# A large and a small expert by turns: eight MoE experts computed as four pairs, on one Trainium2 core

## The chip, the cores and the metric

One core of a Trainium2 chip runs the whole program, one launch. The metric is the device time of a run in microseconds (us). Engines are named as the profile names them: PE is TensorE (PEld its weight loads), DVE is VectorE, ACT is ScalarE, POOL is GpSimd, SP is SyncE, which issues the weight transfers.

## What is computed

A two-layer diffusion backbone on 256 context and 256 latent tokens of width 1024. The change lies in the last part of layer 1, a mixture of eight experts of which every latent token takes the best two. Each expert has three weight matrices in float32, 1024 x 2816 for gate and up, 2816 x 1024 for down:

```python
def swiglu(h, w_gate, w_up, w_down):
    return (jax.nn.silu(h @ w_gate) * (h @ w_up)) @ w_down

def moe_swiglu(h, router_w, w_gate, w_up, w_down):
    logits = (h @ router_w).astype(F32)
    top_v, top_i = lax.top_k(logits, TOP_K)
    top_w = jax.nn.softmax(top_v, axis=-1)
    combine = jnp.sum(jax.nn.one_hot(top_i, N_EXPERTS, dtype=F32) * top_w[..., None], axis=-2)
    out = jnp.zeros(h.shape[:-1] + (w_down.shape[-1],), h.dtype)
    for e in range(N_EXPERTS):
        out = out + combine[..., e:e + 1].astype(h.dtype) * swiglu(h, w_gate[e], w_up[e], w_down[e])
    return out
```

## The kernel before

Expert 0 and the three fullest of the others get 128 token slots, the other four get 64; a ranking on the chip decides which of experts 1 to 7 is computed in which place. Places 0, 2, 4, 6 are the large ones (`expert`), places 1, 3, 5, 7 the small ones (`expert64`). Place 2p and place 2p+1 are pair p. What the program calls expert `e` is a place; `home_of(e)` reads the number of the real expert into a register of SP, whose DMAs use it as address.

**Weights.** Each place takes 33 loads of 128 x 2048 float32 (1 MB): 22 for gate and up, 11 for down. `load` issues them from SP into ten buffers in rotation: seven called `raw`, two `own`, one `whole`. The tile `whole` also holds the small expert's tokens (`xs`) and its activations (`a64`), so a row `whole<-pm` on ACT writes those.

**Large expert.** Six groups, five of four loads and one of two, each 512 (256) columns of gate and up. A load is split for precision in two halves, each into `whi` (ACT, L352) and the rest `wlo` (DVE, L353), three buffers of each, and a k-tile takes three matmuls: high x high, low tokens x high, high x low (L1196 to L1198). A group is 48 matmuls. Its result goes through Silu (ACT, L1201) and the product with up (DVE, L1202) into `a`; later `turned` transposes `a` (PE, L1207) and stores it as `ahi` (ACT, L1209) and `alo` (DVE, L1210). The down loads use the same split and three matmuls (L1232 to L1234) into two PSUM tiles `pd`, one for each half of the output columns.

**Small expert.** The same groups, but its matmuls (L1253) take the weights unsplit in float32, eight to a gate or up load and four to a down load (L1289), two of them beside each other in the array. Silu is L1259, the product L1260, the transposes L1265, their evacuation L1267.

**Around them.** `pick` makes the one-hot matrices of a pair, `gather` (L1147, four matmuls for each of eight k-tiles) collects the tokens of the next pair during the small expert's down loads, `scatter_rows` transposes the one-hots, `scatter` writes a half of an expert's output back: `y` (ACT, L1299, one buffer) and its rest (DVE, L1300), eight matmuls (L1305), four additions (L1308).

**Order.** The places are computed one after the other, all of place 0, then all of place 1, and so on. Which instruction stands where in an engine's list is decided when the program is built, by a scheduler that goes by priorities (the splits are marked high) and by its own estimate of when operands are there. Each engine then works through its list. SP issues the loads in the order of the program, each when its buffer is free.

Of the kernel before, what the change touches and what calls it, by code (L numbers as in the profile page):

```python
# [20 lines left out]
KD = 8  # L21
# [62 lines left out]
def host_layout(x, c, ctx, c_ctx, ada_w, ada_b, mix_norm_w, ffn_norm_w, w_in, hg_lb_logits, hg_norm_w,  # L84
# [95 lines left out]
    "pre": 4,  # L180
    "hold": 5,
    "ff": (1, 1),
    "sg": 1,
    "tt": 2,
    "td": 2,
    "slots": (3, 5, 8),
    "pk": 3,
    "gd": 1,
    "sd": 8,
    "dv": ([], [4, 5, 6, 7, 8, 9, 10, 11, 12, 13, 14, 15, 16, 17, 18]),  # L190
    "al": 2,
    "pc": ((), ()),
# [6 lines left out]
def tile_kernel(ctx: ExitStack, tc: tile.TileContext, xT, cT, cR, ada_w, w_in, w_br, w_out, ffn_gu, ffn_d, router,  # L199
# [29 lines left out]
    def pm(shape=(P, 512)):  # L229
        return pt("pm", n_pm, shape)  # L230
# [928 lines left out]
    def scatter_rows(pr, oh):  # L1159
        ohf = oh.bitcast(F32)  # L1160
        pw = pm((P, 2))
        ws = mt((2,), "ws", 2)
        pt_ = pm((P, 2, 2, P))
        oT = mt((2, 2, P), "oT", 1, F32R)
        for ee in range(2):
            for t in range(2):
                T.matmul(pw[:, ee:ee + 1], ohf[:, t, ee], wgt_s[:, t, 2 * pr + ee:2 * pr + ee + 1],
                         start=t == 0, stop=t == 1)
                T.transpose(pt_[:, ee, t], ohf[:, t, ee], ident)
        V.tensor_copy(ws, pw)  # L1170
        S.activation(oT, pt_, AF.Copy)
        return ws, oT

    def expert(e, oh, st, choose, early):
        pr, ee = divmod(e, 2)
        at_ = home_of(e)
        if ee:
            return expert64(e, at_, oh, st, choose, early)
        xv = [xg[:, s_] for s_ in range(2)]
        aT, turn_ = [], []  # L1180
        for g in range(6):
            w = 512 if g < 5 else 256
            kc = 4 if g < 5 else 8
            pss = []
            for u in range(2):
                ps = pj() if g % 2 else pt(("po", "pa")[u], 1)
                for c in range(8 // kc):
                    n = 4 * g + 2 * u + c if g < 5 else 20 + u
                    raw = load(moe[at_, n]).rearrange("p (k c) -> p k c", k=kc)
                    for k0 in range(0, kc, kc // 2):  # L1190
                        if turn_ and 4 * (kc * c + k0) >= kc * PLAN["tt"]:
                            turn_.pop()()
                        hi, lo = split(raw[:, k0:k0 + kc // 2], (kc // 2, w))
                        for k in range(kc // 2):
                            kk = kc * c + k0 + k
                            T.matmul(ps[:, :w], xv[0][:, kk], hi[:, k], start=kk == 0, stop=False)  # L1196
                            T.matmul(ps[:, :w], xv[1][:, kk], hi[:, k], start=False, stop=False)  # L1197
                            T.matmul(ps[:, :w], xv[0][:, kk], lo[:, k], start=False, stop=kk == 7)  # L1198
                pss.append(ps)
            a = tpool.tile([P, 512], F32, tag="rstd", name=nm("act"))  # L1200
            S.activation(a[:, :w], pss[0][:, :w], AF.Silu)  # L1201
            V.tensor_tensor(a[:, :w], a[:, :w], pss[1][:, :w], ALU.mult)  # L1202

            def turned(a=a, nt=w // P):
                pq = pm((P, 4, P))
                for q in range(nt):
                    T.transpose(pq[:, q], a[:, q * P:(q + 1) * P], ident)  # L1207
                hi, lo = mt((4, P), "ahi", 6, F32R), mt((4, P), "alo", 6, F32R)
                S.activation(hi[:, :nt], pq[:, :nt], AF.Copy)  # L1209
                V.tensor_tensor(lo[:, :nt], pq[:, :nt], hi[:, :nt].bitcast(F32), ALU.subtract)  # L1210
                aT.append((hi, lo))

            turn_.append(turned)
            if g == PLAN["pk"]:
                choose()
            if g == PLAN["sg"]:
                if late:
                    late.pop()()
                st.update(zip(("ws", "oT"), scatter_rows(pr, oh)))
        pd = [pm(), pm()]  # L1220
        for c in range(11):
            raw = load(moe[at_, 22 + c]).rearrange("p (k c) -> p k c", k=4)
            early(c - PLAN["gd"])
            for k in range(4):
                h_, kk = DOWN[4 * c + k]
                if turn_ and 4 * c + k == 2 * PLAN["td"]:
                    turn_.pop()()
                if k % 2 == 0:
                    hi, lo = split(raw[:, k:k + 2], (2, 512))
                ahi, alo = (x[:, kk % 4] for x in aT[kk // 4])  # L1230
                first, last = (kk == 0, kk == 21) if h_ == 0 else (kk == 20, kk == 19)
                T.matmul(pd[h_], ahi, hi[:, k % 2], start=first, stop=False)  # L1232
                T.matmul(pd[h_], alo, hi[:, k % 2], start=False, stop=False)  # L1233
                T.matmul(pd[h_], ahi, lo[:, k % 2], start=False, stop=last)  # L1234
            if c == PLAN["sd"]:
                scatter(e, 0, pd[0], st["ws"], st["oT"])
        late.append(lambda: scatter(e, 1, pd[1], st["ws"], st["oT"]))

    def expert64(e, at_, oh, st, choose, early):


        aT, turn_ = {}, []
        for g in range(6):
            w = 512 if g < 5 else 256
            kc, hw = (4 if g < 5 else 8), w // 2
            ps = pj((P, 2, 256))
            for u in range(2):
                for c in range(8 // kc):
                    raw = load(moe[at_, 4 * g + 2 * u + c if g < 5 else 20 + u]).rearrange("p (k c) -> p k c", k=kc)
                    for k in range(kc):  # L1250
                        kk = kc * c + k
                        for h_ in range(2):
                            T.matmul(ps[64 * h_:64 * h_ + 64, u, :hw], xs[:, kk], raw[:, k, h_ * hw:(h_ + 1) * hw],  # L1253
                                     start=u + kk == 0, stop=u == 1 and kk == 7, tile_position=(0, 64 * h_),
                                     skip_group_check=True)
                    if turn_:
                        turn_.pop()()
            a = tpool.tile([P, 512], F32, tag="rstd", name=nm("act"))[:, :hw]
            S.activation(a, ps[:, 0, :hw], AF.Silu)  # L1259
            V.tensor_tensor(a, a, ps[:, 1, :hw], ALU.mult)  # L1260

            def turned(a=a, g=g, nt=hw // P):
                pq = pm((P, 4, P))
                for q in range(nt):
                    T.transpose(pq[:, q], a[:, q * P:(q + 1) * P], ident)  # L1265
                o = a64[:, g]
                S.activation(o[:, :nt], pq[:, :nt], AF.Copy)  # L1267
                for h_ in range(2):
                    for q in range(nt):
                        aT[4 * g + nt * h_ + q] = o[:, q, 64 * h_:64 * h_ + 64]  # L1270

            turn_.append(turned)
            if g == PLAN["pk"]:
                choose()
            if g == PLAN["sg"] and late:
                late.pop()()
        if e == NE - 1:
            S.activation(mt((1,), "most"), a[:, 0:1], AF.Exp, scale=0.0)
        pd = [pm(), pm()]
        for c in range(11):  # L1280
            raw = load(moe[at_, 22 + c]).rearrange("p (k c) -> p k c", k=4)
            early(c - PLAN["gd"])
            for k in range(4):
                h_, kk = DOWN[4 * c + k]
                if turn_ and c == 1:
                    turn_.pop()()
                r = kk % 2
                first, last = (kk < 2, kk >= 20) if h_ == 0 else (kk >= 20, 18 <= kk < 20)
                T.matmul(pd[h_][64 * r:64 * r + 64], aT[kk], raw[:, k], start=first, stop=last,  # L1289
                         tile_position=(0, 64 * r), skip_group_check=True)  # L1290
            if c == PLAN["sd"]:
                scatter(e, 0, pd[0], st["ws"], st["oT"])
        late.append(lambda: scatter(e, 1, pd[1], st["ws"], st["oT"]))

    def scatter(e, h_, pd, ws, oT):
        ee = e % 2
# [10 lines left out]
                x = xl[4 * h_ + m + q]  # L1307
                V.scalar_tensor_tensor(x, ps[:, q], mods[1][:, 40 + 4 * h_ + m + q, 0:1], x, ALU.mult, ALU.add)  # L1308

    late, ohs = [], [pick(0)]  # L1310
    for k in range(KD):
        gather(k, ohs[0], True)
    for pr in range(4):
        st = {}
        for ee in range(2):
            def choose():
                if ee and pr < 3:
                    ohs.append(pick(pr + 1))

            def ahead(k):  # L1320
                if ee and pr < 3 and 0 <= k < KD:
                    gather(k, ohs[pr + 1], False)

            expert(2 * pr + ee, ohs[pr], st, choose, ahead)
    late.pop()()
    more["own"] = []


# [109 lines left out]
```

## Time and profile before

| | us |
|---|---|
| median of 3 runs | 2152.09 (2151.23 to 2155.42) |
| profiled execution, its own time | 2149.9 |
| its span | 2147.7 |
| first matmul of place 0 | 1442.76 |
| last matmul of place 7 begins | some 2126 |
| PE, DVE, ACT busy over the span | 96%, 61%, 43% |
| mean granted TensorE clock | 0.987 of full speed |

The expert stage is the last third of the span. The span counts from the first to the last instruction; the execution's own time lies 2.2 us above it. Busy PE counts matmuls whose ends are modelled and which overlap, so the share says little: where PE is slowed by something, it is seen by the distance between the starts of matmuls. In rows, "[1.73 <-ACT whi L352]" means that the engine was idle for 1.73 us before the row, and that ACT's instruction of line 352 ended that. The DMA and GB/s figures are of the 16 DMA engines together.

### The profile page before, as it was taken

The numbers are of one execution on the slowest core, as the hardware profiler recorded it, in microseconds if no ns is written. First come the engines' busy times: TensorE is split into PE (matmuls) and PEld (weight loads), VectorE is DVE, ScalarE is ACT, GpSimd is POOL, SyncE is SP. The second block draws the span as 40 slices with busy tenths as digits, with TensorE's granted clock in tenths as the row PEclk, the third lists the DMA queues.
The fourth block names the chain that finished last, engine by engine and source line by source line (L and its number), as shares of the span: only waits on it lengthen the run. The fifth ranks groups of instructions, "written<-read, shape, count | busy, mean of one in ns | idle before, by whom it ended". The sixth has DMA issues, their size and how long they took to land. (4 is left out here: it accounts for less than half of the span.)

```text
span 2147.7 us, 34454 instructions
## 1 busy us (share of the span) xinstructions
PE 2061.4 (96%) x13828; PEld 1577.5 (73%) x13828; DVE 1303.1 (61%) x2362; ACT 926.9 (43%) x1424; POOL 35.3 (2%) x101
## 2 busy tenths in 40 slices
PE   6999999999989999999999999989999999999997
PEld 3777777777868878887778878878758756855863
DVE  7677456664465468534777777669619717915931
ACT  3653233322344222223755443448527616715821
POOL 0000000010000000000000000000000000000000
PEclk9999999999999999999999999989999999999998
DMA  8341413112262446322333223369999999999995
GB/s 329 122 157 61 175 61 118 40 61 79 99 254 98 137 160 253 128 68 95 109 111 118 102 99 110 132 237 364 365 421 421 381 422 419 363 405 421 375 389 224
DMA packets 66983, 455.45 MB, mean 212 GB/s; under 512 B 7680, under 2 KB 8192, under 8 KB 13952
## 3 DMA queue, kind: packets, MB, share of 16 engines
q1 hardware_dynamic: 64224, 447.78, 54.0%
q10 hardware_dynamic: 2592, 5.41, 0.7%
q8 instruction: 110, 1.80, 0.3%
q14 instruction: 57, 0.47, 0.1%
HBM read 452.11 MB, written 1.05 MB: 211 GB/s over the span
## 5 line engine op out<-in xcount | busy, mean ns | idle before, releaser
L352 ACT ACTIVATE whi<-raw 128x1024 fp32r<-128x1024 f32 (+3 forms) x442 | 436.2, 993 | 575.8 <-PE pj L360 495.8
L353 DVE TENSOR_TENSOR wlo<-raw,whi 128x1024 fp32r<-128x1024 f32 (+3 forms) x442 | 497.4, 1140 | 215.2 <-ACT whi L352 204.4
L359 PE MATMUL pj<-hhi,whi 128*128 128x512 f32 (+1 forms) x1216 | 452.3, 373 | 10.4 <-ACT hhi L487 9.6
L361 PE MATMUL pj<-hhi,wlo 128*128 128x512 f32 (+1 forms) x1216 | 451.3, 372 | 0.4 <-DVE wlo L353 0.4
L360 PE MATMUL pj<-hlo,whi 128*128 128x512 f32 (+1 forms) x1216 | 450.1, 371 | 0.2 <-DVE hlo L488 0.2
L359 PEld LDWEIGHTS pj<-hhi,whi 128*128 128x128 f32 x1216 | 230.6, 190 | 52.4 <-ACT hhi L487 12.3
L361 PEld LDWEIGHTS pj<-hhi,wlo 128*128 128x128 f32 x1216 | 230.5, 190 | 40.5 <-issue 5.4
L360 PEld LDWEIGHTS pj<-hlo,whi 128*128 128x128 f32 x1216 | 230.7, 190 | 39.2 <-issue 3.0
L1253 PE MATMUL pj<-raw,whole 128*64 128x256 f32 (+1 forms) x1088 | 114.4, 362 | 0.0
L1260 DVE TENSOR_TENSOR act<-act,pj 128x256 f32<-128x256 f32 (+1 forms) x24 | 9.6, 398 | 156.6 <-ACT act L1259 156.6
L1253 PEld LDWEIGHTS pj<-raw,whole 128*64 128x64 f32 x1088 | 73.5, 137 | 33.2 <-issue 2.6
L1259 ACT ACTIVATE act<-pj 128x256 f32<-128x256 f32 (+1 forms) x24 | 8.8, 366 | 144.2 <-PE pj L1253 144.2
L359 PE MATMUL pj<-yhi,whi 128*128 128x512 f32 (+1 forms) x192 | 66.8, 350 | 3.4 <-ACT yhi L513 3.1
L361 PE MATMUL pj<-ahi,wlo 128*128 128x512 f32 x176 | 69.2, 393 | 0.3 <-DVE wlo L353 0.3
L359 PE MATMUL pj<-ahi,whi 128*128 128x512 f32 x176 | 69.1, 393 | 0.0
L1232 PE MATMUL pm<-whi,ahi 128*128 128x512 f32 x176 | 69.0, 392 | 0.0
L1197 PE MATMUL pj<-whi,xg 128*128 128x512 f32 (+1 forms) x192 | 68.8, 359 | 0.0
L1233 PE MATMUL pm<-whi,alo 128*128 128x512 f32 x176 | 68.6, 390 | 0.0
L360 PE MATMUL pj<-alo,whi 128*128 128x512 f32 x176 | 68.5, 389 | 0.0
L1196 PE MATMUL pj<-whi,xg 128*128 128x512 f32 (+1 forms) x192 | 68.4, 356 | 0.2 <-ACT whi L352 0.2
L1234 PE MATMUL pm<-wlo,ahi 128*128 128x512 f32 x176 | 68.2, 390 | 0.0
L1198 PE MATMUL pj<-wlo,xg 128*128 128x512 f32 (+1 forms) x192 | 68.0, 354 | 0.0
(362 smaller groups left out, 3609.6 us busy)
## 6 DMA issues: line engine op xcount, KB each, us to landing
raw<-in_moe_dram SPq DMA_DIRECT2D x185, 1024.0 KB, 9.4
raw<-in_w_in_dram SPq DMA_DIRECT2D x58, 1024.0 KB, 4.9
own<-in_moe_dram SPq DMA_DIRECT2D x53, 1024.0 KB, 9.3
raw<-in_ada_w_dram SPq DMA_DIRECT2D x44, 1024.0 KB, 4.9
whole<-in_moe_dram SPq DMA_DIRECT2D x26, 1024.0 KB, 9.1
raw<-in_ffn_gu_dram SPq DMA_DIRECT2D x22, 1024.0 KB, 4.8
raw<-in_w_br_dram SPq DMA_DIRECT2D x12, 1024.0 KB, 4.9
raw<-in_ffn_d_dram SPq DMA_DIRECT2D x16, 704.0 KB, 4.1
```

The source lines that it names most:

```text
L352: S.activation(hi, src, AF.Copy)
L353: V.tensor_tensor(lo, src, hi.bitcast(F32), ALU.subtract)
L359: T.matmul(ps, whi(k), hhi(k), start=first and k == 0, stop=False)
L360: T.matmul(ps, whi(k), hlo(k), start=False, stop=False)
L361: T.matmul(ps, wlo(k), hhi(k), start=False, stop=last and k == n - 1)
L1196: T.matmul(ps[:, :w], xv[0][:, kk], hi[:, k], start=kk == 0, stop=False)
L1197: T.matmul(ps[:, :w], xv[1][:, kk], hi[:, k], start=False, stop=False)
L1198: T.matmul(ps[:, :w], xv[0][:, kk], lo[:, k], start=False, stop=kk == 7)
L1232: T.matmul(pd[h_], ahi, hi[:, k % 2], start=first, stop=False)
L1233: T.matmul(pd[h_], alo, hi[:, k % 2], start=False, stop=False)
L1234: T.matmul(pd[h_], ahi, lo[:, k % 2], start=False, stop=last)
L1253: T.matmul(ps[64 * h_:64 * h_ + 64, u, :hw], xs[:, kk], raw[:, k, h_ * hw:(h_ + 1) * hw], start=u + kk == 0, stop=u == 1 and kk == 7, tile ...
```

## The change

Both experts of a pair become generators and `pair` draws from them by turns: in gate and up one group of the large, one group of the small; in down one load of each. In pair 0 the turns follow a string of their own (three large groups first). The transposes of a group wait in one common list `turn_` and are called during the next group, of whichever expert. The down results move from the PSUM tiles `pm` to `po`, `pa` and `pj`. Scatters of the second output halves of both experts are done in the first two turns of the next pair, those of the first halves after down load 7 of each, the gathers of the next pair after each turn of down loads 1 to 8.

```diff
-    "sg": 1,
     "tt": 2,
-    "td": 2,
     "slots": (3, 5, 8),
-    "pk": 3,
+    "pk": 7,
     "gd": 1,
-    "sd": 8,
+    "sd": 7,
+    "first": "BBBSSBSBSBSS",
...
-    def expert(e, oh, st, choose, early):
-        pr, ee = divmod(e, 2)
+    turn_, late = [], []
+
+    def do_turn():
+        if turn_:
+            turn_.pop()()
+
+    def expert(e):
...
-                        if turn_ and 4 * (kc * c + k0) >= kc * PLAN["tt"]:
-                            turn_.pop()()
+                        if 4 * (kc * c + k0) >= kc * PLAN["tt"]:
+                            do_turn()
...
-            if g == PLAN["sg"]:
-                if late:
-                    late.pop()()
-                st.update(zip(("ws", "oT"), scatter_rows(pr, oh)))
-        pd = [pm(), pm()]
+            yield
+        pd = [None, None]
         for c in range(11):
             raw = load(moe[at_, 22 + c]).rearrange("p (k c) -> p k c", k=4)
-            early(c - PLAN["gd"])
...
+                if pd[h_] is None:
+                    pd[h_] = pj() if h_ else pt("po", 1)
...
-            if c == PLAN["sd"]:
-                scatter(e, 0, pd[0], st["ws"], st["oT"])
-        late.append(lambda: scatter(e, 1, pd[1], st["ws"], st["oT"]))
-
-    def expert64(e, at_, oh, st, choose, early):
+            yield pd
+
+    def expert64(e):
...
-                    if turn_:
-                        turn_.pop()()
+                    do_turn()
...
+                if pd[h_] is None:
+                    pd[h_] = pj() if h_ else pt("pa", 1)
...
+    def pair(pr):
+
+        both = expert(2 * pr), expert64(2 * pr + 1)
+        rows = None
+        for n, who in enumerate(PLAN["first"] if pr == 0 else "BS" * 6):
+            next(both["BS".index(who)])
+            if late:
+                scatter(*late.pop(0))
+            elif rows is None:
+                rows = scatter_rows(pr, ohs[pr])
+            if n == PLAN["pk"] and pr < 3:
+                ohs.append(pick(pr + 1))
+        for c in range(11):
+            for ee in range(2):
+                e, pd = 2 * pr + ee, next(both[ee])
+                if c == PLAN["sd"]:
+                    scatter(e, 0, pd[0], *rows)
+                if c == 10:
+                    late.append((e, 1, pd[1], *rows))
+            if pr < 3 and 0 <= c - PLAN["gd"] < KD:
+                gather(c - PLAN["gd"], ohs[pr + 1], False)
...
     for pr in range(4):
...
+        pair(pr)
+    for rest in late:
+        scatter(*rest)
```

How this moves instructions is seen in the lists of the engines. ACT before, in the large expert of pair 1, around the end of its third group (`act_14850` is that group's Silu, `ahi_14870` the evacuation of the second's transposes, `whi` the splits of the loads that follow):

```order
L1201 ACTIVATE act_14850<-po_14752 128x512
L352 ACTIVATE whi_14830<-raw_14828 128x1024
L352 ACTIVATE whi_14840<-raw_14828 128x1024
L352 ACTIVATE whi_14855<-own 128x1024
L352 ACTIVATE whi_14874<-own 128x1024
L352 ACTIVATE whi_14886<-raw_14884 128x1024
L352 ACTIVATE whi_14896<-raw_14884 128x1024
L1209 ACTIVATE ahi_14870<-pm_14865 128x512
```

Two loads of the next group (from `own` on) are split ahead of the evacuation of this one's transposes. ACT after the change, in pair 1, at the end of the second turn (`act_14785` is the Silu of the large group, `act_14851` that of the small one, `whole<-pm_14867` the evacuation of the small group's transposes):

```order
L1205 ACTIVATE act_14785<-pj_14692 128x512
L351 ACTIVATE whi_14765<-raw_14763 128x1024
L351 ACTIVATE whi_14775<-raw_14763 128x1024
L1213 ACTIVATE ahi_14817<-pm_14812 128x512
L1255 ACTIVATE act_14851<-pj_14802 128x256
L1263 ACTIVATE whole<-pm_14867 128x256
L351 ACTIVATE whi_14857<-raw_14855 128x1024
L351 ACTIVATE whi_14871<-raw_14855 128x1024
```

`raw_14763` is the last load of the large group of this turn; the first of the next, `raw_14855`, is split behind the small group's Silu and the evacuation of its transposes. PE at the same place (`pj_14802` is the small group's result, `po_14854` that of the next large group):

```order
L1202 MATMUL pj_14740<-wlo_14776,xg_13119 128x512
L1250 MATMUL pj_14802<-own,whole 64x256 x8
L1211 MATMUL pm_14812<-cc,act_14785 128x128 x4
L1250 MATMUL pj_14802<-raw_14821,whole 64x256 x8
L1250 MATMUL pj_14802<-raw_14831,whole 64x256 x8
L1250 MATMUL pj_14802<-raw_14841,whole 64x256 x8
L1261 MATMUL pm_14867<-cc,act_14851 128x128 x2
L1200 MATMUL po_14854<-whi_14857,xg_13119 128x512
L1201 MATMUL po_14854<-whi_14857,xg_13119 128x512
```

The transposes of the large group stand behind the first small load; those of the small group stand directly between its last matmul and the next large group's first.

## Rows read from the trace of the kernel before

**Rows 1.** Windows, expert stage: length, busy PE PEld DVE ACT POOL, clock, DMA share, GB/s

```profile
1450.00:1550.00 100.00, 99.82 (x533) 80.69 (x533) 82.10 (x84) 69.98 (x76) 0.00 (x0) 1.00 0.95 360
1550.00:1680.00 130.00, 125.77 (x775) 88.39 (x772) 72.75 (x91) 68.27 (x96) 0.00 (x0) 1.00 1.01 421
1450.00:2120.00 670.00, 646.12 (x3907) 466.28 (x3907) 383.84 (x445) 342.51 (x445) 0.00 (x0) 0.99 0.99 396
```

**Rows 2.** What the SP queue waited for, 1450 to 2120: total us, times, longest

```profile
SPq L343 <- DVE wlo L353: 204.3, 85, 3.7
```

**Rows 3.** Windows, the four pairs: first large matmul to the next pair's

```profile
1442.76:1611.64 168.88, 165.00 (x995) 117.99 (x994) 96.93 (x118) 88.83 (x123) 0.00 (x0) 1.00 0.94 370
1611.64:1784.41 172.77, 165.72 (x1002) 119.07 (x1002) 98.87 (x118) 89.36 (x120) 0.00 (x0) 1.00 1.00 408
1784.41:1958.67 174.26, 167.21 (x1001) 120.18 (x1001) 98.96 (x118) 89.33 (x120) 0.00 (x0) 0.99 0.99 398
1958.67:2126.02 167.35, 161.45 (x969) 116.63 (x969) 94.94 (x104) 80.37 (x94) 0.00 (x0) 0.99 0.96 381
```

**Rows 4.** Timeline of PE, large expert of pair 0: start us, duration us, engine

```profile
1478.55 0.39 PE L1196 MATMUL pj<-whi,xg 128*128 128x512 f32 x1
...
1480.13 0.66 PE L1207 MATMUL pm<-cc,act 128*128 128x128 f32 x4
...
1481.09 0.40 PE L1196 MATMUL pj<-whi,xg 128*128 128x512 f32 x1
...
1489.73 0.39 PE L1198 MATMUL pj<-wlo,xg 128*128 128x512 f32 x1
...
1501.37 0.28 PE L1196 MATMUL pj<-whi,xg 128*128 128x256 f32 x1
...
1507.64 0.40 PE L1232 MATMUL pm<-whi,ahi 128*128 128x512 f32 x1
```

**Rows 5.** Timeline of PE, small expert of pair 0

```profile
1540.71 1.90 PE L1253 MATMUL pj<-raw,whole 128*64 128x256 f32 x16
...
1544.16 3.62 PE L1253 MATMUL pj<-raw,whole 128*64 128x256 f32 x32
1547.72 0.44 PE L1265 MATMUL pm<-cc,act 128*128 128x128 f32 x2
```

**Rows 6.** Timeline of PE, a scatter in the down loads of pair 0

```profile
1532.42 1.11 PE L1305 MATMUL pm<-oT,y 128*128 128x256 f32 x8
1533.37 0.40 PE L1232 MATMUL pm<-whi,ahi 128*128 128x512 f32 x1
```

**Rows 7.** Line 343, the load issued at 1587.4: forms, and time to landing

```profile
L343 SPq DMA_DIRECT2D raw<-in_moe_dram x1: 333/333/333, 1587.4 to 1587.4; - x1
...
DMA to landing us min/median/max: 17.5/17.5/17.5
```

**Rows 8.** Timeline of all engines, from pair 0 to pair 1

```profile
1609.96 0.69 ACT L1299 ACTIVATE y<-pm,ws 128x512 fp32r<-128x512 f32 x1 [5.67 <-PE pm L1289]
1610.54 2.94 ACT L352 ACTIVATE whi<-raw 128x1024 fp32r<-128x1024 f32 x3
...
1611.64 0.50 PE L1196 MATMUL po<-whi,xg 128*128 128x512 f32 x1 [1.73 <-ACT whi L352]
...
1612.90 0.50 PE L1198 MATMUL po<-wlo,xg 128*128 128x512 f32 x1 [0.53 <-DVE wlo L353]
```

**Rows 9.** Timeline of ACT and DVE, small expert, end of its first group

```profile
1546.11 0.38 ACT L1259 ACTIVATE act<-pj 128x256 f32<-128x256 f32 x1 [6.38 <-PE pj L1253]
1546.52 0.42 DVE L1260 TENSOR_TENSOR act<-act,pj 128x256 f32<-128x256 f32 x1 [6.01 <-ACT act L1259]
...
1548.19 0.38 ACT L1267 ACTIVATE whole<-pm 128x256 f32<-128x256 f32 x1 [1.70 <-PE pm L1265]
```

**Rows 10.** Windows at the starts of pairs 2 and 3

```profile
1780.00:1790.00 10.00, 7.74 (x29) 4.39 (x26) 5.79 (x6) 5.08 (x6) 0.00 (x0) 0.83 1.01 420
...
1960.00:1970.00 10.00, 10.00 (x38) 8.11 (x39) 7.62 (x7) 7.07 (x8) 0.00 (x0) 0.86 1.01 419
```

More of the change, by code (lines that the diff above doesn't have):

```diff
@@ L1172, in scatter_rows @@
         return ws, oT
-    def expert(e, oh, st, choose, early):
-        pr, ee = divmod(e, 2)
+    turn_, late = [], []
[3 more added lines that the diff above has]
+    def expert(e):
         at_ = home_of(e)
-        if ee:
-            return expert64(e, at_, oh, st, choose, early)
         xv = [xg[:, s_] for s_ in range(2)]
-        aT, turn_ = [], []
+        aT = []
         for g in range(6):
@@ L1213, in expert @@
             turn_.append(turned)
-            if g == PLAN["pk"]:
-                choose()
-            if g == PLAN["sg"]:
-                if late:
-                    late.pop()()
-                st.update(zip(("ws", "oT"), scatter_rows(pr, oh)))
-        pd = [pm(), pm()]
+            yield
+        pd = [None, None]
         for c in range(11):
             raw = load(moe[at_, 22 + c]).rearrange("p (k c) -> p k c", k=4)
-            early(c - PLAN["gd"])
             for k in range(4):
                 h_, kk = DOWN[4 * c + k]
-                if turn_ and 4 * c + k == 2 * PLAN["td"]:
-                    turn_.pop()()
                 if k % 2 == 0:
                     hi, lo = split(raw[:, k:k + 2], (2, 512))
+                if pd[h_] is None:
+                    pd[h_] = pj() if h_ else pt("po", 1)
                 ahi, alo = (x[:, kk % 4] for x in aT[kk // 4])
@@ L1234, in expert @@
                 T.matmul(pd[h_], ahi, lo[:, k % 2], start=False, stop=last)
-            if c == PLAN["sd"]:
-                scatter(e, 0, pd[0], st["ws"], st["oT"])
-        late.append(lambda: scatter(e, 1, pd[1], st["ws"], st["oT"]))
-    def expert64(e, at_, oh, st, choose, early):
-        aT, turn_ = {}, []
+            yield pd
+    def expert64(e):
+        at_ = home_of(e)
+        aT = {}
         for g in range(6):
@@ L1255, in expert64 @@
                                      skip_group_check=True)
-                    if turn_:
-                        turn_.pop()()
+                    do_turn()
             a = tpool.tile([P, 512], F32, tag="rstd", name=nm("act"))[:, :hw]
@@ L1272, in expert64 @@
             turn_.append(turned)
[L1273 to L1276, printed above, removed]
+            yield
         if e == NE - 1:
             S.activation(mt((1,), "most"), a[:, 0:1], AF.Exp, scale=0.0)
-        pd = [pm(), pm()]
+        pd = [None, None]
         for c in range(11):
             raw = load(moe[at_, 22 + c]).rearrange("p (k c) -> p k c", k=4)
-            early(c - PLAN["gd"])
+            do_turn()
             for k in range(4):
                 h_, kk = DOWN[4 * c + k]
-                if turn_ and c == 1:
-                    turn_.pop()()
+                if pd[h_] is None:
+                    pd[h_] = pj() if h_ else pt("pa", 1)
                 r = kk % 2
@@ L1290, in expert64 @@
                          tile_position=(0, 64 * r), skip_group_check=True)
-            if c == PLAN["sd"]:
-                scatter(e, 0, pd[0], st["ws"], st["oT"])
-        late.append(lambda: scatter(e, 1, pd[1], st["ws"], st["oT"]))
+            yield pd
     def scatter(e, h_, pd, ws, oT):
@@ L1308, in scatter @@
                 V.scalar_tensor_tensor(x, ps[:, q], mods[1][:, 40 + 4 * h_ + m + q, 0:1], x, ALU.mult, ALU.add)
-    late, ohs = [], [pick(0)]
+    def pair(pr):
[18 more added lines that the diff above has]
+                gather(c - PLAN["gd"], ohs[pr + 1], False)
+    ohs = [pick(0)]
     for k in range(KD):
@@ L1313, in tile_kernel @@
     for pr in range(4):
[L1314 to L1325, printed above, removed]
+        pair(pr)
+    for rest in late:
+        scatter(*rest)
     more["own"] = []
```

## The prediction

> **What bounds the kernel now.** I read the delivery of weights first, by stretches [rows 1]. From 1550 to 1680 us the transfers run at 421 GB/s, and no stretch of the expert stage is clearly above that; a load is 1.049 MB, so 2.49 us at that rate. From 1450 to 1550, while the first large expert is computed, they run at 360, and over 1450 to 2120 at 396: 670 x (1 - 396/421) = 39.8 us of transfer time are given away, nearly all of it in large experts. The reader is to see a stage that is bound by TensorE in large experts (the SP queue waits longest for VectorE's part of a split to free a buffer [rows 2]) and by transfers in small ones.
>
> Then the length of each pair, from the first large matmul to the next pair's [rows 3]: 168.9, 172.8, 174.3 and 167.4 us, 683.3 in all. The transfers of a pair need 66 x 2.49 = 164.4.
>
> Then TensorE's own work. In a large group the matmuls follow each other every (1489.73 - 1481.09)/38 = 0.227 us; between 1480.13 and 1481.09 stand four transposes and two matmuls, so four transposes cost 0.96 - 0.45 = 0.5; the sixth group, 48 half-wide matmuls and its transposes, takes 6.27, so 5.8 without them [rows 4]. A large load of twelve matmuls is 2.72 us, more than its transfer. A small load takes (1544.16 - 1540.71)/2 = 1.725 [rows 5], less than its transfer. A scatter is eight matmuls in 0.95, 0.119 each [rows 6].
>
> Work of a pair: 372 x 0.227 = 84.4, and 5.8; 33 small loads at 1.725 = 56.9 (a down load has the same number of columns); large transposes 2.8; 32 gather and 32 scatter matmuls at 0.119 = 7.6 (gathers are narrower: upper end). Together **157.5 us**, under the 164.4 of the transfers. So turns could hide one behind the other, if nothing else waits.
>
> **Where it waits after the change.** The order of the instructions decides. Before, the splits of the next large loads stand on ScalarE ahead of the previous group's evacuation `ahi`, and TensorE always has the next half load. After, in pairs 1 to 3, ScalarE's list for each turn is: Silu of the small group, evacuation of its transposes, and only then the first split of the next large group; on TensorE the small transposes stand between the last small matmul and the first large one. That is one chain with nothing beside it.
>
> Does a split wait behind something in front of it though its load is there? In today's trace, yes: the 67th load of the stage, the first of the second pair, is issued at 1587.45 and lands 17.5 us later, at 1604.9 [rows 7]; its split starts at 1610.54, because `y` stands ahead of it and waits for TensorE until 1609.96 [rows 8]. That spot occurs three times now. The change has fifteen more like it.
>
> The price of one, from rows. The small group's last matmul leaves its slot at 1544.16 + 1.725 = 1545.89. Silu starts 0.22 later, the product 0.41 after that and lasts 0.42 [rows 9]. The transposes can start some 0.05 later (today a small load stands between). From their start to their evacuation is 0.47 (1547.72 to 1548.19) [rows 5, 9]. The split follows about 0.3 later (as 1610.54 follows 1609.96, less the difference in length), TensorE starts 1.10 after it, and the third matmul, which needs the VectorE half, 1.26 after that, though the two before it take 0.45 [rows 8]. Sum: 0.22 + 0.41 + 0.42 + 0.05 + 0.47 + 0.30 + 1.10 + 0.81 = **3.8 us** per change from small to large, 5 a pair.
>
> A full turn is then 48 x 0.227 + 0.5 + 4 x 1.725 + 3.8 = 22.1 us for eight loads, whose transfers need 19.9. The transfers wait for TensorE, so the loads are there and nothing hides the chain. That is also why the chain can't be charged to slow delivery.
>
> One rule speaks to this. The Trainium skill, "DMA: Bandwidth & Descriptors", section "Where 436 GB/s comes from", holds that the memory side binds a load at about 358 GB/s. By it a load would need 2.93 us, a turn 23.4, and the chain would cost nothing; by it today's pairs would also need 193 us each. The trace disagrees with 421 GB/s for 130 us [rows 1], and pairs of 167 to 174 [rows 3], so no chance is set on it.
>
> **The change part by part.**
> - Turns in pairs 1 to 3: 157.5 + 5 x 3.8 = 176.5. From the last small group to the down loads the splits stand right behind the Silu: third matmul 0.22 + 0.30 + 1.10 + 1.26 = 2.9 after the small group, less 0.7 of work inside it: 2.2. From down to the next pair: between 0.8 (the 2.94 from `y` to the third matmul [rows 8], less a small load and two matmuls beside it) and today's idle times of 1.73 + 0.53 [rows 8]; I take 1.4, the middle, as a scatter's adds now precede the split on VectorE. Pair: **180.1**; the last one has no gathers: 176.3.
> - Pair 0 has its own order and, unlike the others, three half loads split ahead at two of its three changes to large. Work 157.5, less 1.9 (its second scatters fall into pair 1), and 0.9 for the rows of its scatter and 1.8 for four small transposes, which elsewhere hide in the chain; waits: 1.2 at the start (1442.76 to 1478.55 for 34.6 us of work [rows 3, 4]), 2.1 before the sixth large group, 3.6 before the down loads, 1.4 at its end: **166.6**.
> - Sum: 166.6 + 2 x 180.1 + 176.3 = 703.1 against 683.3: +19.8.
> - Tail: two late scatters in place of one after the last load; the second's `y` has one buffer and waits for the first's matmuls: 0.95 and a hand-over of 0.15 [rows 6]: +1.1.
> - Nothing for: `pd` in other PSUM banks (each is read before the next but one use), `pick` later (behind eight groups), reading expert 1's number before the 13th load (its value is long written when buffers first come free), scatters moved within a pair (the same matmuls; hidden where the chain waits, and if not, at most 1 us each).
>
> +20.9 on the profiled execution's 2149.9 gives 2170.8; the median of the runs is 2.2 above that execution: **2173 us**.
>
> Bounds of the chain: below, today's idle at such a spot, 2.26 [rows 8], and the transposes of 0.44 that the chain holds [rows 5]: 2.7, 15 x 1.1 less: 2157. Above, with a fall of the clock: at two of the three spots of today the granted clock reads 0.83 and 0.86 for 10 us [rows 10], about 3 us at 1.2 GHz, 1.7 lost; 15 of these are +25: 2198. I take 3.8 because each of its links has a row of its own.
>
> **Rivals.**
> - *Faster: the turn is bound by transfers.* If the split doesn't wait for the small group (the lists run otherwise than I read them, or a link is far shorter), delivery stays at 421 after the first three large groups, which still run at some 360 (4.6 us lost, and about 2 until the queue fills again). 39.8 - 6.7 = 33 us are won: 2119. For it: work 157.5 under 164.4, and ten buffers that carry a turn's swing of one load. Against it: the lists. It decides at 1.6 us per change (19.9 less the turn's 18.3 of other work); at some 2.3 a pair takes what it takes today, at 3.8 it is the forecast.
> - *Much slower: the clock falls at each change*, as above: 2198. For it: two of three spots. Against: today the matmuls before those spots wait for transfers; in the turns they are dense, and after 1610 us, the third, the clock stayed at full.
> - *No change*: the chain is shorter still, some 2.4, and gain and loss cancel: 2152.
>
> **How the numbers follow.** Forecast 0.59, own range 2154 to 2192; faster rival 0.28, spread from 2112 up to 2147 by what is left of the chain; clock 0.08; no change 0.05. The range from 2128 to 2197 leaves out the lower half of the faster rival and little above. A measurement tells 0.2% (4 us). Faster 0.28, same 0.06, slower 0.66.
>
> **What would show it.** Right: ScalarE rows in pairs 1 to 3 in the order Silu, `whole<-pm`, split, TensorE idle before each large group's first matmul with the split as its releaser, some 3 us; delivery near 385 GB/s all through pairs 1 to 3, with no stretch at 421 for long; SP waiting for buffers. Pair lengths near 180. Wrong: delivery at 420 from 1490 us on and a last load near 2087; then the chain was not on the path. A clock below 0.95 all over the stage would show the second rival.

## The result and the profile after the change

The changed kernel takes **2245.36 us** (median of 4 runs, 2244.7 to 2248.8) beside 2153.76 for the kernel before on the same chip: ratio 1.0428, 95% interval 1.0413 to 1.0443. Forecast were 2173, range 2128 to 2197. The direction was right; the loss is 92 us, where 21 was forecast.

The four pairs of the changed kernel by windows, each from its first large matmul to the next pair's (the last to its last small matmul), as in [rows 3]; below them the gate and up part and the down part of pair 1, then one large and one small part of a turn:

```profile
1444.64:1621.83 177.19, 171.10 (x995) 117.78 (x995) 94.70 (x113) 86.86 (x122) 0.00 (x0) 0.99 0.94 377
1621.83:1822.77 200.94, 183.17 (x1003) 123.36 (x1002) 100.75 (x118) 86.47 (x119) 0.00 (x0) 0.95 0.91 345
1822.77:2024.05 201.28, 183.18 (x1003) 123.43 (x1002) 100.71 (x118) 86.46 (x119) 0.00 (x0) 0.95 0.91 345
2024.05:2219.96 195.91, 177.70 (x963) 118.44 (x961) 97.75 (x105) 78.51 (x94) 0.00 (x0) 0.95 0.82 308
...
1621.83:1759.23 137.40, 121.47 (x729) 87.53 (x727) 67.16 (x77) 54.59 (x69) 0.00 (x0) 0.93 0.90 338
1759.23:1822.77 63.54, 61.70 (x274) 35.82 (x275) 33.59 (x42) 31.88 (x51) 0.00 (x0) 1.00 0.94 361
...
1673.00:1687.00 14.00, 13.47 (x54) 10.25 (x55) 9.86 (x9) 7.32 (x8) 0.00 (x0) 0.88 0.86 321
1687.00:1697.00 10.00, 7.64 (x66) 4.55 (x63) 1.27 (x4) 2.36 (x5) 0.00 (x0) 1.00 0.95 377
```

Forecast for the pairs were 166.6, 180.1, 180.1 and 176.3: 10.6, 20.8, 21.2 and 19.6 too little, 72 together. Delivery in pairs 1 and 2 is 345 GB/s, where 385 was forecast and the kernel before had 408 and 398 [rows 3]. In a turn the granted clock is below full in the large part and full in the small one. The transfers wait for the engines: the SP queue (1450 to 2220) waits for buffers that VectorE's part of a split holds, for 189.2 us on the line that answers to [rows 2], and next for buffers that the small matmuls hold:

```profile
SPq L342 <- DVE wlo L352: 189.2, 62, 5.4
SPq L342 <- PE pj L1250: 100.5, 54, 3.4
```

One change from small to large in pair 1, timeline of all engines without weight loads; what answers to [rows 5, 8, 9]:

```profile
1692.31 1.90 PE L1250 MATMUL pj<-raw,whole 128*64 128x256 f32 x16
...
1694.25 0.38 ACT L1255 ACTIVATE act<-pj 128x256 f32<-128x256 f32 x1 [4.74 <-PE pj L1250]
1694.67 0.42 DVE L1256 TENSOR_TENSOR act<-act,pj 128x256 f32<-128x256 f32 x1 [4.43 <-ACT act L1255]
...
1695.14 0.44 PE L1261 MATMUL pm<-cc,act 128*128 128x128 f32 x2 [0.94 <-DVE act L1256]
1695.62 0.38 ACT L1263 ACTIVATE whole<-pm 128x256 f32<-128x256 f32 x1 [0.98 <-PE pm L1261]
1695.90 2.94 ACT L351 ACTIVATE whi<-raw 128x1024 fp32r<-128x1024 f32 x3
...
1697.00 0.50 PE L1200 MATMUL pj<-whi,xg 128*128 128x512 f32 x1 [1.42 <-ACT whi L351]
...
1698.26 0.62 PE L1202 MATMUL pj<-wlo,xg 128*128 128x512 f32 x1 [0.53 <-DVE wlo L352]
...
1701.24 0.63 PE L1200 MATMUL pj<-whi,xg 128*128 128x512 f32 x1
...
1702.24 0.39 PE L1200 MATMUL pj<-whi,xg 128*128 128x512 f32 x1
...
1703.61 0.39 PE L1200 MATMUL pj<-whi,xg 128*128 128x512 f32 x1
```

The chain reads link by link as forecast: Silu, product, transposes, evacuation, split, each released by the one before. From the end of the last small load (its start plus the 1.725 of [rows 5], 1692.31 + 1.725 = 1694.04) to the third large matmul are 4.22 us, 0.45 of them work of the first two large matmuls and 3.8 chain. What was not in the forecast comes behind it: from 1698.26 to 1701.24 seven matmuls follow each other every 0.426 us, the lower of the two clock levels (1.2 GHz), and from 1702.24 to 1703.61 six every 0.228, the upper one (2.4). Eight slow ones cost 8 x 0.2 = 1.6 us. A turn is 1697.00 (this change's first large matmul) - 1672.80 (the one a turn earlier) = 24.2 us; forecast 22.1.

In the down loads, timeline of PE, pair 1, one turn without a stall:

```profile
1784.03 0.40 PE L1231 MATMUL po<-whi,alo 128*128 128x512 f32 x1
1784.26 0.39 PE L1232 MATMUL po<-wlo,ahi 128*128 128x512 f32 x1
1784.58 1.94 PE L1282 MATMUL pa<-raw,whole 128*64 128x512 f32 x8
1786.45 0.50 PE L1230 MATMUL po<-whi,ahi 128*128 128x512 f32 x1
1786.79 0.40 PE L1231 MATMUL po<-whi,alo 128*128 128x512 f32 x1
```

TensorE waits for nothing here, and yet a small load takes 1.87 us where it took 1.725 among its like [rows 5], the step from the last large matmul to it 0.32 instead of 0.23, and the first large matmul after it 0.34 instead of 0.23: 0.09 + 0.145 + 0.11 = some 0.35 a turn, each time the shape of the tile on the array changes from 128 columns to 64 and back. The large and the small matmuls also differ in their number format, which these rows can't tell from the shape; E5 can.

### The profile page after: what moved, and what is told of

It is laid out like the page before. It is cut to its first block, busy times and chain, and to the rows that moved or that the text cites. A ratio compares the mean times of both kernels' runs of the same rounds, so it can differ in the third digit from the quotient of the medians.

```text
span 2243.8 us, 34363 instructions
## 1 busy us (share of the span) xinstructions
PE 2120.6 (95%) x13828; PEld 1589.4 (71%) x13828; DVE 1309.3 (58%) x2362; ACT 917.3 (41%) x1424; POOL 35.3 (2%) x101
## 5 line engine op out<-in xcount | busy, mean ns | idle before, releaser
L351 ACT ACTIVATE whi<-raw 128x1024 fp32r<-128x1024 f32 (+2 forms) x454 | 444.2, 992 | 609.8 <-PE pj L359 490.3
L352 DVE TENSOR_TENSOR wlo<-raw,whi 128x1024 fp32r<-128x1024 f32 (+2 forms) x454 | 512.2, 1143 | 269.4 <-ACT whi L351 261.0
L1200 PE MATMUL pj<-whi,xg 128*128 128x512 f32 (+1 forms) x192 | 76.1, 396 | 9.4 <-ACT whi L351 9.3
L1202 PE MATMUL pj<-wlo,xg 128*128 128x512 f32 (+1 forms) x192 | 76.5, 398 | 7.5 <-DVE wlo L352 7.5
L1201 PE MATMUL pj<-whi,xg 128*128 128x512 f32 (+1 forms) x192 | 74.7, 389 | 0.0
L352 DVE TENSOR_TENSOR wlo<-own,whi 128x1024 fp32r<-128x1024 f32 x52 | 62.1, 1221 | 19.3 <-ACT whi L351 18.2
L359 PE MATMUL pj<-ylo,whi 128*128 128x512 f32 (+1 forms) x192 | 66.5, 347 | 0.0
L360 PE MATMUL pj<-yhi,wlo 128*128 128x512 f32 (+1 forms) x192 | 66.3, 346 | 0.0
L351 ACT ACTIVATE whi<-own 128x1024 fp32r<-128x1024 f32 x52 | 53.6, 1054 | 18.8 <-PE pj L1201 7.4
L1213 ACT ACTIVATE ahi<-pm 128x512 fp32r<-128x512 f32 (+1 forms) x24 | 13.5, 561 | 116.0 <-PE pm L1211 115.9
```

The source lines that it names most:

```text
L351: S.activation(hi, src, AF.Copy)
L352: V.tensor_tensor(lo, src, hi.bitcast(F32), ALU.subtract)
L359: T.matmul(ps, whi(k), hlo(k), start=False, stop=False)
L360: T.matmul(ps, wlo(k), hhi(k), start=False, stop=last and k == n - 1)
```

## The experiments

The theories. A: the chain of waits is the cost. B: the clock falls behind it, for some 1.7 us more. C: the down loads by turns cost by the change of tile shape and by splits that stand behind `y`. Rival R: transfers that alternate between two places are slower, and TensorE's idle time is only where that shows. Times are medians of four runs (ten for E9 and E10), ratios are to the kernel before.

| | edit to the changed kernel | us | ratio (95%) |
|---|---|---|---|
| E1 | first load of the next large group split ahead | 2246.33 | 1.0412 to 1.0461 |
| E2 | down loads one expert after the other | 2231.38 | 1.0346 to 1.0384 |
| E3 | gate and up one expert after the other | 2185.37 | 1.0128 to 1.0171 |
| E4 | turns of two groups in pairs 1 to 3 | 2210.09 | 1.0258 to 1.0292 |
| E5 | matmuls that fill the gap | 2227.13 | 1.0318 to 1.0358 |
| E6 | first scatters after down load 9 | 2242.14 | 1.0404 to 1.0442 |
| E7 | three half loads ahead, order fixed | 2174.33 | 1.0090 to 1.0124 |
| E8 | E7 and E2 | 2166.28 | 1.0054 to 1.0089 |
| E9 | E7, large transposes behind a small load | 2155.33 | 0.9996 to 1.0018 |
| E10 | E9 and E2 | 2145.26 | 0.9962 to 0.9982 |
| E11 | E10, next pair's splits ahead of `y` | 2138.18 | 0.9913 to 0.9962 |
| E12 | two down loads a turn | 2253.31 | 1.0437 to 1.0490 |

**E1.** At the end of each large group, before its `yield`:

```diff
+        def fetch(g):
...
+            got.append((raw, [split(raw[:, k0:k0 + kc // 2], (kc // 2, w)) for k0 in range(0, kc, kc // 2)]))
...
+            fetch(g + 1)
             yield
```

> The first load of the next large group is issued, and both its halves split, before the small group's turn. Theory A (the chain Silu, transposes, evacuation, first split stands on the path at each change from small to large, 3.1 us of idle TensorE, and the clock falls behind it for some 1.7 us more): a turn falls from 24.2 us to some 20 (its eight transfers need 19.9), 4 us x 15 turns in pairs 1 to 3 are saved: 2245 - 60 = about 2185; granted clock 1.0 in the turns. Rival R (the turns are slow because transfers that alternate between two places run at some 360 GB/s, and TensorE's idle time is only where that shows): the wait moves to the raw buffers, 2245 within 10. Rival S (each change of tile shape on TensorE costs some tenths): TensorE's list now mixes small loads and large halves, two to four more changes per turn, so less is saved than by A: 2195 to 2225.

Nothing was saved, as R has it. But the timeline of PE in pair 1 shows another reason:

```profile
1685.17 1.95 PE L1266 MATMUL pj<-raw,whole 128*64 128x256 f32 x16
...
1688.23 0.40 PE L1212 MATMUL pj<-whi,xg 128*128 128x512 f32 x1
1688.56 1.95 PE L1266 MATMUL pj<-own,whole 128*64 128x256 f32 x16
...
1697.46 0.44 PE L1277 MATMUL pm<-cc,act 128*128 128x128 f32 x2 [0.94 <-DVE act L1272]
1699.31 0.79 PE L1212 MATMUL pj<-whi,xg 128*128 128x512 f32 x1 [1.42 <-ACT whi L351]
```

The scheduler put the early large matmuls (L1212 to L1214) between the small loads (L1266), so that none was left beside the chain, and the split of the next half load stands behind it as before: 0.94 and 1.42 us of idle time, unchanged. The run leaves A, R and S open.

**E2.**

```diff
-        for c in range(11):
-            for ee in range(2):
+        for ee in range(2):
+            for c in range(11):
```

> Gate and up by turns as in the change, the down loads one expert after the other, gathers among the small one's. Theory C (the down phase by turns costs 63 to 65 us a pair instead of 56.5: 0.4 us per turn for the change of tile shape and 2.3 twice for a split that stands behind y): about 7 us a pair less, 4 pairs, 2245 - 26 = about 2219, a down phase near 57 us. Rival: the down phase is bound by its 22 transfers (54.8 at 2.49) plus the two changes of pair, and sequential order leaves a large part bound by TensorE and a small part by transfers: 2240 to 2250.

14 us were won, about half of what C promised; the down phase of pair 1 is 62.1 us instead of 63.5. The last pair's, which has no gathers, falls by 4.2 (59.3 to 55.1, from the first large down matmul to the last small one), about the eleven turns' 0.35. In the other pairs the gathers now stand between small loads, with a change of shape on either side, so that most of that cost stays.

**E3.** `"BS" * 6` becomes `"BBBBBBSSSSSS"`, in pair 0 too.

> Gate and up one expert after the other (six large groups, then six small), the down loads by turns as in the change. Theory A with the clock: 15 changes of small to large vanish, gate and up fall from 137 us to 110 to 113 (44 transfers need 109.6): 3 x 25 less: about 2170, and the granted clock in gate and up is 1.0 but for a place at the pair's start. If only the idle 3.1 us of each change were the cost, and the clock fell for another reason: 2245 - 46 = 2199. Rival R (transfers slower when two places alternate): the down phase, which still alternates, stays at 360 GB/s, and gate and up run at 421: also near 2170, but then E1 shows no gain.

60 us less, 15 less than theory A expected. Gate and up of pair 1 take 116.07 instead of 137.40 at a clock of 1.00 (110 to 113 were expected); the down phase, 63.54 in the changed kernel, takes 64.78. So the turns in gate and up hold most of the loss. The down loads still alternate, and at 400 GB/s, which speaks against R.

```profile
1619.17:1735.24 116.07, 108.61 (x732) 82.21 (x731) 65.08 (x77) 56.32 (x70) 0.00 (x0) 1.00 0.96 378
1735.24:1800.02 64.78, 62.84 (x272) 36.52 (x273) 33.60 (x42) 31.91 (x50) 0.00 (x0) 0.97 0.99 400
```

**E4.** `"BS" * 6` becomes `"BBSSBBSSBBSS"` for pairs 1 to 3.

> Turns of two groups in pairs 1 to 3 (two large, two small, and so on), pair 0 as in the change: the changes from small to large within gate and up fall from 5 a pair to 2, 9 fewer in all. Theory A with B: each is 3.1 us idle and 1.7 of slow clock, 9 x 4.8 = 43 less: about 2202. If the turn is bound by slow transfers: 2240 to 2248.

35 us less for 9 changes fewer: 3.9 each, where chain and clock together are 5.4 (3.8 and 1.6). The loss goes with the number of changes. The trace shows the rest: behind a small group that another small group follows, TensorE still waits 0.94 us for the product before the transposes, and these still take 0.44 (pair 1, at 1655.38, 1699.44 and 1738.06): 5.4 - 0.94 - 0.44 = 4.0.

**E5.** Four matmuls per gap, whose results nobody reads:

```diff
+                for k in range(1):
+                    T.matmul(idle[:, 0], ident, t, start=True, stop=True)
...
+                    for k in range(3):
+                        T.matmul(idle[:, 1], ident, o.rearrange("p q c -> p (q c)"), start=True, stop=True)
```

> The change as it is, with four more float32 matmuls (128 x 256, results never used) in each gap between a small and a large group: one that needs Silu's output, three that need the evacuation of the transposes. The chain keeps its length, TensorE is no longer idle for more than about 1 us of it. Theory B (the clock falls because TensorE stands idle some 3 us, and that costs 1.6 to 1.8 us per turn beside the chain): the first matmuls of each large group follow each other every 0.227 us instead of 0.427, a turn is 22.5 us instead of 24.2, 15 x 1.7 = 25 less: about 2220. If the fall has nothing to do with the idle gap: 2245 to 2250.

Timeline of PE at the same change, and the window of gate and up in pair 1 (L1260 and L1275 are the added matmuls):

```profile
1699.93 0.70 PE L1260 MATMUL pm<-t,cc 128*128 128x256 f32 x2 [0.48 <-ACT t L1257]
1700.47 0.38 PE L1270 MATMUL pm<-cc,act 128*128 128x128 f32 x2
...
1701.33 1.56 PE L1275 MATMUL pm<-whole,cc 128*128 128x256 f32 x6 [0.47 <-ACT whole L1272]
...
1702.54 0.58 PE L1200 MATMUL pj<-whi,xg 128*128 128x512 f32 x1
...
1703.87 0.40 PE L1200 MATMUL pj<-whi,xg 128*128 128x512 f32 x1
...
1704.56 0.39 PE L1200 MATMUL pj<-whi,xg 128*128 128x512 f32 x1
...
1631.41:1760.01 128.60, 120.85 (x769) 88.49 (x768) 66.70 (x77) 54.77 (x69) 0.00 (x0) 1.00 0.95 362
```

The matmuls behind the gap follow each other every 0.23 us at once, the clock reads 1.00 instead of 0.93, and gate and up fall by 137.40 - 128.60 = 8.8 us: 1.76 for each of five changes. The chain keeps its length (from the start of the last small load, 1697.56, plus 1.725 to the third large matmul, 1703.53, are 4.24 us, before 4.22). B is shown, and its price. In the total 18 us instead of 25 were won: in the profiled run the expert stage began 4.4 us later, behind work that the edit doesn't touch, and pair 0 took 5 us longer; why was not looked for.

The same run tells shape from number format for C. In a turn of pair 1 some of the added matmuls, float32 as the small loads are but of 128 columns, landed between large ones (timeline of PE):

```profile
1657.28 1.02 PE L1275 MATMUL pm<-whole,cc 128*128 128x256 f32 x4
1657.95 0.58 PE L1200 MATMUL pj<-whi,xg 128*128 128x512 f32 x1
1658.37 0.40 PE L1201 MATMUL pj<-whi,xg 128*128 128x512 f32 x1
```

The four follow each other every 0.215 us and start 0.23 behind the large matmul ahead of them; from their start to the second large one behind them are 1.09 us, four times 0.215 and one 0.23. A change of number format at the same shape costs nothing here.

**E7.** Three half loads are split ahead of the small group's turn (two in E1), and the order of issue is pinned:

```diff
+            while len(got) < 3:
+                got.append(next(each))
+            mark["dve"] = newest(mybir.EngineType.DVE)
+            mark["act"] = newest(mybir.EngineType.Activation)
...
+                            with behind("pe"):
+                                T.matmul(ps[:, :w], xv[0][:, kk], hi[:, k], start=kk == 0, stop=False)
...
+            mark["pe"] = newest(mybir.EngineType.PE)
+            with behind("act"):
+                S.activation(a, ps[:, 0, :hw], AF.Silu)
```

> As E1 with three half loads ahead, and with the order of issue fixed: Silu of the small group stands behind those three splits on ScalarE, its product behind them on VectorE, and the first matmul of the next large group behind the small group's last one on TensorE, so that 12 to 18 large matmuls lie beside Silu, product, transposes and evacuation. Theory A (E1 saved nothing because TensorE's list took the early halves before the chain instead of beside it; the chain itself is the cost): turns of 18.6 to 20 us instead of 24.2 (eight transfers need 19.9), granted clock 1.0, delivery near 421 in gate and up; 15 x 4.2 to 5 saved: 2170 to 2185. Rival R (transfers that alternate between two places run at 360 GB/s): turns of 23.3, about 2230, with ScalarE's splits waiting for the loads.

71 us less, inside A's range, and against R: the turns still alternate between two places, and gate and up deliver 379 GB/s. Timeline in pair 1, first the change from small to large, then the one from large to small, and the window of gate and up:

```profile
1679.69 1.47 PE L1276 MATMUL pj<-raw,whole 128*64 128x256 f32 x12
1681.09 0.50 PE L1225 MATMUL pj<-whi,xg 128*128 128x512 f32 x1
1681.20 0.38 ACT L1283 ACTIVATE act<-pj 128x256 f32<-128x256 f32 x1 [6.47 <-PE pj L1276]
...
1682.58 0.38 PE L1290 MATMUL pm<-cc,act 128*128 128x128 f32 x2
...
1692.15 0.39 PE L1227 MATMUL pj<-wlo,xg 128*128 128x512 f32 x1
...
1693.96 0.66 PE L1236 MATMUL pm<-cc,act 128*128 128x128 f32 x4 [1.42 <-DVE act L1231]
...
1617.02:1733.56 116.54, 108.18 (x727) 81.63 (x725) 70.17 (x78) 57.67 (x69) 0.00 (x0) 1.00 0.93 379
```

Large matmuls now run beside Silu and product, and the transposes (L1290) come six matmuls later with no idle time. A new wait has taken its place: the large group's transposes (L1236) stand ahead of the first small load and wait 1.42 us for their product. In the changed kernel they stand behind it.

**E9.** That wait undone:

```diff
-                    do_turn()
+                    with tc.issue_after(newest(mybir.EngineType.PE)):
+                        do_turn()
```

> E7, with the large group's transposes issued behind the small group's first load on TensorE (in E7 they stand ahead of it and wait 1.6 us for the product). TensorE's turn falls from 20.5 to some 19.0, under the 19.9 of its eight transfers. Theory: the turn is then bound by transfers at 19.9, 15 x 0.6 = 9 less than E7, about 2165, or up to 15 x 1.5 = 22 less if loads that are ahead cover it: 2152 to 2166. The down phase by turns stays near 62. Rival (the wait of 1.6 is only moved to the next group): 2174.

The turn is 1679.83 - 1660.66 = 19.2 us, delivery 421 GB/s over 80 us of turns, TensorE without a pause. That settles R: transfers that alternate between two places run at the 421 of [rows 1]. All pairs are still computed by turns, and the time is that of the kernel before, within 0.2%. Below, the start of a turn, the start of the next, the window of the turns, and gate and up and the down phase of pair 1.

```profile
1660.66 0.50 PE L1225 MATMUL po<-whi,xg 128*128 128x512 f32 x1
...
1679.83 0.50 PE L1225 MATMUL pj<-whi,xg 128*128 128x512 f32 x1
...
1660.00:1740.00 80.00, 80.00 (x528) 58.68 (x525) 44.23 (x44) 40.59 (x53) 0.00 (x0) 1.00 1.01 421
...
1617.94:1728.50 110.56, 109.38 (x727) 81.06 (x725) 70.53 (x78) 57.72 (x69) 0.00 (x0) 1.00 0.96 397
1728.50:1790.21 61.71, 60.62 (x280) 35.87 (x279) 30.58 (x40) 30.52 (x50) 0.00 (x0) 1.00 1.01 421
```

**E6 and E12, two misses among the down loads.** E6: `"sd": 9`. E12: two down loads of one expert per turn.

> One number: the scatters of the first halves after down load 9 instead of 7. Theory C (y stands on ScalarE ahead of the next splits while it waits for the last matmuls of po, 2.3 us twice a pair): y comes when po is long finished, no turn of 7.1 us is left among the down loads, 8 x 2.3 = 18 less: about 2227. Rival: the wait only moves to the next place, or the long turns have another cause: 2240 to 2248.

> The change with two down loads of one expert per turn instead of one: 5 fewer turns among the down loads of a pair. If each turn there pays for the change of tile shape on TensorE (a small load takes 1.87 instead of 1.72, the matmul after each side comes 0.1 late: 0.36 in all), the down phase falls by 5 x 0.36 = 1.8 us, from 57.5 to 55.7 in the last pair, which has no gathers, and by 2 to 4 where gathers are gathered in longer rows too: 4 pairs, 2245 - 10 = about 2235. If only the waits behind y make it long: the last pair stays at 57 to 58, and 2240 to 2247.

E6 takes 1 us off a down phase (63.54 to 62.57), not 4.6: `y` is the smaller part of C. E12 is slower as a whole. Where nothing waits, in the last pair, a turn of two loads of each is 9.38 us from start to start, two turns of one load 2 x 4.87: 0.36 saved, the price of the shape change; the whole phase there falls by 1.4 (57.5 to 56.2), where 1.8 was expected. But in pair 1 the phase grew from 63.5 to 68.3, and TensorE's idle time in it from 1.8 to 4.8. Little of that is behind `y` (0.78 us). For 3.5 of it ScalarE's list has the evacuation of a gather (L1154) ahead of the next large splits, and the gather stands on TensorE behind both small loads. All engines, pair 1, the longer of the two places:

```profile
1781.35 0.46 ACT L1154 ACTIVATE x<-pm,mods,coef 128x128 f32<-128x128 f32 x1 [6.25 <-PE pm L1146]
...
1782.80 0.50 PE L1230 MATMUL po<-whi,ahi 128*128 128x512 f32 x1 [1.49 <-ACT whi L351]
```

It is the same kind of chain as in gate and up, at another place.

**E8, E10 and E11.** E8 and E10 are E7 and E9 with the loop of E2. E11 issues the next pair's first splits at the last down load, and the last `y` behind them:

```diff
+                if pr < 3 and ee == 1 and c == 10:
+                    nexts.append(expert(2 * pr + 2))
+                    next(nexts[0])
+                    mark["y"] = newest(mybir.EngineType.Activation)
```

> E7 with the down loads one expert after the other, as in E2. If the two causes add up: E7 less what E2 saved (14 us), about 2160 to 2168. If gate and up then run at the transfers' rate and leave the buffers full, the down phase has more to gain than in E2 (its large part starts with ten loads there): 2140 to 2155, at or under the kernel before. If the order of E7 does nothing: 2231 as E2.

> E9 with the down loads one expert after the other (as E8 is to E7). E8's pairs take 176.8 and deliver at 420 from the first turn of pair 1 on but for its starts. Theory: pairs near 170 (66 transfers need 164.4), 3 x 6 less than E8: 2140 to 2152, level with the kernel before or a little under. Rival: bound by TensorE in the down phase as well, 2155 to 2166.

> E10, with the first three half loads of the next pair split before the last y on ScalarE. The idle time at a pair's start (2.3 us from the last down matmul to the first large one in E8) falls below 1: 3 x 1.5 = 4 less than E10 if TensorE sets the end there, nothing (within 3 us) if transfers do.

Down loads one after the other are worth 8 us (E8) and 10 us (E10). E11 wins 7 more, with no idle TensorE at the start of pairs 1 and 2, and is the fastest version: ratio 0.9938 to the kernel before (0.9913 to 0.9962). Its pairs 1 and 2:

```profile
1613.16:1781.55 168.39, 168.39 (x1003) 118.52 (x1001) 101.54 (x118) 89.22 (x119) 0.00 (x0) 1.00 1.00 415
1781.55:1949.95 168.40, 168.40 (x1004) 118.52 (x1002) 101.56 (x118) 89.18 (x119) 0.00 (x0) 1.00 0.99 411
```

TensorE and the transfers are both busy all the time, and a pair takes 168.4. Whether the last trick would help the kernel before as well was not tried.

## Why the prediction was right in direction and wrong in size

- **The order of the lists decides: right.** Breaking the chain (E7) and the wait that it uncovered (E9) gives 90 us back with the same work and the same turns, the clock's share among them.
- **The chain of 3.8 us: right**, link by link and in sum.
- **The clock: here the prediction failed.** It gave the fall at each change to a rival with a chance of 0.08 and put nothing for it into the sum, since the matmuls in the turns are dense and one of today's three places kept its clock. What counted was the idle time ahead of them: some 3 us with 0.44 of transposes in it, and with matmuls put into it the clock stayed (E5). The rival's own price, 1.7 us per change and 25 us in all, was right: E5 measured 1.76, so 15 changes are 26 us of the 72. Its total, 2198, lay 47 us too low all the same.
- **A pair's work of 157.5: too low**, the second step that failed, and the larger one. E9 computes pair 1 by turns at a clock of 1.00, and TensorE is busy there for 109.38 + 60.62 = 170.0 us, 12.5 more. By the distances from start to start, idle time taken off, 5.1 of that are in the large matmuls, 3.8 in the small loads, 1.0 in gathers and scatters, 0.5 in the large transposes; the other 2.1 are the small transposes and those of the one-hots, which the forecast had hidden in the chain. So 10.4 were missing. Matmul pitch and load times were read from stretches of one tile shape; each turn pays for changes of shape, 0.35 us among the down loads, some 0.5 in gate and up, where the large transposes stand between two small loads: 11 x 0.35 + 5 x 0.5 = some 6 a pair. That this is the price of the shape is shown for the down loads (E12, E5); in gate and up it is read from the steps. The other 4 were not taken apart; 0.8 is the down phase's large matmuls, which follow each other every 0.233 us instead of 0.227.
- **The down phase** was priced at 56 (132 x 0.227, 11 x 1.725, gathers, two scatters, 1.4) and is 63.5: 4 of the 7.5 are shape changes, 1 is `y` (E6), 0.8 the pitch. The rest was not taken apart.
- **The sum for pair 1**, 20.8 over the forecast: 8.8 clock, 10.4 work, 1 `y`; 0.6 stays unassigned.
- **The faster rival** (2119, bound by transfers) needed a pair's work under 164.4. By turns it is 170.0 (E9), with the down loads in sequence 168.4 (E11), and the best version reaches 2138. In E9 delivery is at 421 GB/s through the turns, as the rival had it; the rule of the Trainium skill ("DMA: Bandwidth & Descriptors", "Where 436 GB/s comes from"), about 358 GB/s, is not borne out here either.
- **Pair 0** is 177.2 against 166.6. Its own order spared it most of the clock (0.99), and TensorE is idle in it for 177.19 - 171.10 = 6.1 us, where the forecast had 8.3 of waits. So its excess is work too: TensorE is busy for 168.7 us of it in E9 (1448.05 to 1617.94), 10.4 above the forecast's 157.5 - 1.9 + 0.9 + 1.8 = 158.3, the same as in pair 1.
- **The tail**: from the last small matmul to the end 2243.8 - 2219.96 = 23.8 us, before 21.7, forecast 22.8.

## What to carry to other kernels

Work that alternates between two parts on engines that go through their lists in order needs the next part's operands prepared before the current part's last results are evacuated, and here also the order pinned on every engine: in E1 issuing early alone only moved the work, in E7 a repaired wait uncovered the next one. When a chain of waits leaves TensorE idle for microseconds, add to its length the slow matmuls behind it, from rows of the same kernel. And before two kinds of matmul are interleaved, price the change between them from a row where they meet, not from stretches of either.

## What the hardware showed that was not expected

- The granted clock fell behind the gaps of the changed kernel's turns, and not where 2 us of otherwise useless matmuls lay in it (E5): added work made the kernel 18 us faster. The gap of 1.42 us at the other change of E7 left the clock at 1.00.
- A change of tile shape on TensorE from 128 columns to 64 and back costs 0.35 us among the down loads (0.36 by E12): 0.09 on the way to 64 columns, the rest on the way back. A change of number format at the same shape cost nothing (E5). The Trainium skill, "TensorEngine Tiling (Array Packing)", section "Key Properties", says that a change of tiling mode drains the engine, without a figure; the longer steps on both sides of a small load fit that.
